# Choice of experts: its steps queued behind the low parts of weights, bounds repeated four times, no low part on GpSimd

## The chip, the cores and the metric

One core of one Trainium2 chip runs the whole program. The metric is device time in microseconds, the median of the runs: 1494.61 us before (three runs, 1493.63 to 1494.88).

## The reference, cut to what matters

Two residual blocks on 256 tokens of width 1024, in float32. The first has a token mixer and then `peer`, a layer that picks 16 of 16384 experts for each token and each of 8 heads. The change lies in `peer`:

```python
q = (ht @ wq).reshape(T, P_HEADS, 2, P_DKH)
s = jnp.einsum('thcd,hcnd->thcn', q, subkeys).astype(jnp.float32)
s1, i1 = lax.top_k(s[:, :, 0], P_TOPK)
s2, i2 = lax.top_k(s[:, :, 1], P_TOPK)
cand = (s1[..., :, None] + s2[..., None, :]).reshape(T, P_HEADS, P_TOPK * P_TOPK)
sc, ci = lax.top_k(cand, P_TOPK)
e = take_along_axis(i1, ci // P_TOPK) * N_KEYS + take_along_axis(i2, ci % P_TOPK)
g = jax.nn.softmax(sc, axis=-1)
# a = gelu(u[e] . h) * g ;  out = sum of a * v[e]
```

The kernel does not gather rows of u and v. It multiplies the tokens with all of u, weighs every expert by the sum of its g (zero for one that was not picked), and multiplies with all of v.

## The kernel before, in words

**Weights.** A float32 product is made as three matmuls of float32r halves: high weight by high input, high weight by low input, low weight by high input (`mm3`, lines 185 to 187). Weights come in by SP's DMA queue as 1 MB pieces `raw` (line 152, three buffers), each of two chunks of 128 x 1024. `split` (lines 160 to 167) makes a chunk's high part `wh` on ACT (line 165) and its low part `wl` = raw - wh on DVE (line 166), or on GpSimd for the chunks listed in `pool_`. In this stretch there are four buffers of each of wh and wl, in a ring. One chunk is 24 matmuls of 128x256 (`gemm`).

**The stretch that the change touches.** The input hh, hl is finished by `modulated` (lines 349, 342, 343) while `gemms` multiplies the first three chunks of u with it (lines 220, 221, 225). Then, for four groups hq of two heads, `queries(hq)` multiplies four chunks of wq (none for the first group, done earlier), copies the product to qT (lines 1022, 1026) and makes two tiles of scores `scs` by 16 matmuls (line 1030) and two ACT copies (line 1033; three buffers). After each group come seven chunks of u (`z_chunks`, up to chunk 28), and then the chunks up to ZR = 50. Each of these ends in a GELU on ACT (line 871). From chunk 50 on, the next background work (`weights_of`, lines 1043 to 1073) needs the chosen indices.

**The choice of experts** runs on DVE beside these chunks, as one generator `routing()`. For each of the eight score tiles, `route` does four steps of MAX8, FIND_INDEX8, MATCH_REPLACE8, MAX8, FIND_INDEX8 (lines 883 to 888), one step that makes 54 candidates a head (lines 895, 899), and two steps like the first four on the candidates (lines 905 to 910). After each second group, `select` turns positions into indices for 128 tokens and four heads: it compares with 16 bounds (`reached`, line 931), multiplies with steps (line 940) or sizes (line 947), and adds up 16 values in four halvings (`total`, lines 936, 937). `spread` makes the softmax (ACT Exp, line 971), turns indices and weights by PE (lines 984, 987) and writes idxT and gT.

**The order.** The program is traced in the order of the code, and a planner then sets each engine's queue by its own costs and the order of tracing; it may put a step that is ready ahead of instructions that were traced before it. `advance` traces NR = 1.6 steps of the generator after each chunk of u, whatever a step takes. `tc.issue_after(ins)` makes what is traced inside it on the engine of `ins` follow `ins` in that engine's queue.

The chunks of u with even numbers below 50 have their low part on GpSimd:

```python
cu = chunks(a["uT"], range(64), pool_={*range(0, 50, 2)})
```

Of the kernel before, what the change touches and what calls it, by code (L numbers as in the profile page):

```python
# [10 lines left out]
F16 = mybir.dt.float16  # L11
# [3 lines left out]
ALU = mybir.AluOpType  # L15
# [20 lines left out]
F2 = 10  # L36
KA = 0
KB = 2
NZ, NR, NW, ZR, NX, NY = (7, 1.6, 1.4, 50, 1.05, 1.05)

# [26 lines left out]
def constants():  # L69
    c = {t: np.zeros((128, n), np.float32) for t, n in NCST.items()}  # L70

    def at(n):
        t, a, w = CST[n]
        return c[t][:, a:a + w]

    p = np.arange(128)
    at("ident")[:] = np.eye(128)
    at("mneg")[:] = np.where(p[:, None] <= p[None, :], 0.0, NEG)
    at("mneg2")[:] = np.where(p[:, None] < p[None, :], 0.0, NEG)
    at("tri")[:] = np.where(p[:, None] >= p[None, :], 1.0, 0.0)  # L80

    at("eh")[:, [7, 39]] = 1.0
    for h in range(8):
        at("dup")[64 + h, [h, 32 + h]] = 1.0
        at("sel")[[h, 32 + h], h] = 1.0
    for i in range(2):
        at("e2")[64 * i:64 * i + 64, [38 + i, 102 + i]] = 1.0
        for m in range(8):
            r = 32 * (m // 4) + 2 * (m % 4) + i
            at("sel2")[[r, 64 + r], 2 * m + i] = 1.0  # L90
    i16 = np.repeat(np.arange(128), TB)[None, :].repeat(128, 0).astype(np.float16)
    start, size = np.zeros(16), np.zeros(16)
    start[1:8] = np.cumsum([n for _, n in RUNS])[:7]
    start[8:] = sum(n for _, n in RUNS) + np.arange(8)
    size[1:] = np.diff(start)
    pick = np.stack([start, size, np.arange(16)])[None].repeat(128, 0).astype(np.float16)
    return c, np.ascontiguousarray(i16), pick.reshape(128, 3 * 16)


class Banks:  # L100
# [12 lines left out]
def body(ctx: ExitStack, tc: tile.TileContext, a: dict):  # L113
# [46 lines left out]
    def split(raw, on=V, by=A):  # L160
        sps.append(sps.pop(0))
        n = sps.count(sps[0])
        wh = sps[0].tile([128, 1024], F32R, tag="wh", name="wh", bufs=n)
        wl = sps[0].tile([128, 1024], F32R, tag="wl", name="wl", bufs=n)
        by.copy(wh, raw) if by is A else by.tensor_copy(wh, raw)  # L165
        on.tensor_sub(wl, raw, wh)  # L166
        return wh, wl

    def chunks(src, blocks, ready=(), late={}, pool_=()):

# [192 lines left out]
    def advance(gens, n=1):  # L363
        due[0] += n
        for _ in range(int(due[0])):
            due[0] -= 1
            while gens:
                try:
                    next(gens[0])
                    break  # L370
                except StopIteration:
                    gens.pop(0)

    def drain(gens):
        while gens:
# [37 lines left out]
    with ExitStack() as p1:  # L413
# [149 lines left out]
        bg = []  # L563
# [268 lines left out]
    with ExitStack() as p2:  # L832
# [43 lines left out]
        def route(t, hq, st):  # L876

            sc = st
            tv = rp.tile([128, 4, 16], F32, tag="tv", name="tv", bufs=2)
            ti = i12[t].rearrange("p h c k -> p (h c) k")[:, 4 * hq:4 * hq + 4]  # L880
            for i in range(4):
                s1 = sc[:, i * 128:(i + 1) * 128]
                V.max(out=tv[:, i, 0:8], in_=s1)
                V.max_index(out=ti[:, i, 0:8], in_max=tv[:, i, 0:8], in_values=s1)
                rep = rp.tile([128, 128], F32, tag="rep", name="rep", bufs=2)
                V.match_replace(out=rep, in_to_replace=tv[:, i, 0:8], in_values=s1, imm_value=-3e38)
                V.max(out=tv[:, i, 8:16], in_=rep)
                V.max_index(out=ti[:, i, 8:16], in_max=tv[:, i, 8:16], in_values=rep)
                yield
            tv2 = tv.rearrange("p (h c) k -> p h c k", c=2)  # L890
            cand = rp.tile([128, 2, NC50], F32, tag="cand", name="cand", bufs=2)
            o = 0
            for lo, hi in GROUPS:
                m, n = hi - lo, 16 // (lo + 1)
                V.tensor_add(cand[:, :, o:o + m * n].rearrange("p h (a b) -> p h a b", a=m),
                             tv2[:, :, 0, lo:hi, None].to_broadcast([128, 2, m, n]),
                             tv2[:, :, 1, None, 0:n].to_broadcast([128, 2, m, n]))
                o += m * n
            V.tensor_add(cand[:, :, o:o + 8], tv2[:, :, 0, 8:16], tv2[:, :, 1, 0:1].to_broadcast([128, 2, 8]))
            yield  # L900
            cv = gw[t][:, 2 * hq:2 * hq + 2, :]
            ci = pos[t][:, 2 * hq:2 * hq + 2, :]
            for i in range(2):
                s1 = cand[:, i, :]
                V.max(out=cv[:, i, 0:8], in_=s1)
                V.max_index(out=ci[:, i, 0:8], in_max=cv[:, i, 0:8], in_values=s1)
                rep = rp.tile([128, 128], F32, tag="rep", name="rep", bufs=2)
                V.match_replace(out=rep[:, :NC50], in_to_replace=cv[:, i, 0:8], in_values=s1, imm_value=-3e38)
                V.max(out=cv[:, i, 8:16], in_=rep[:, :NC50])
                V.max_index(out=ci[:, i, 8:16], in_max=cv[:, i, 8:16], in_values=rep[:, :NC50])  # L910
                yield

        def select(t, q):

# [7 lines left out]
            V.tensor_copy(cf, pos[t][:, hs, :].rearrange("p h k -> p k h"))  # L922
            V.tensor_copy(st[:, :, 0], tf[:, :, 0])
            V.tensor_sub(st[:, :, 1:16], tf[:, :, 1:16], tf[:, :, 0:15])
            yield
            m = rp.tile([128, 16, 16, 4], F16, tag="m", name="m", bufs=1)
            pr = rp.tile([128, 16, 16, 4], F16, tag="pr", name="pr", bufs=1)
            mf, pf = (v_.rearrange("p a k h -> p a (k h)") for v_ in (m, pr))

            def reached(at, v_):  # L930
                V.tensor_tensor(out=mf, in0=v_.rearrange("p k h -> p (k h)")[:, None, :].to_broadcast([128, 16, 64]),
                                in1=pick[:, at, :, None].to_broadcast([128, 16, 64]), op=ALU.is_ge)

            def total(out):
                for n in (8, 4, 2):
# [4 lines left out]
                V.tensor_tensor(out=pr, in0=m, in1=st[:, c, :, None, :].to_broadcast([128, 16, 16, 4]), op=ALU.mult)  # L940

            reached(0, cf)
            steps(0)
            yield
            total(fi[t][:, 0, 64 * q:64 * q + 64])
            yield
            V.tensor_tensor(out=pf, in0=mf, in1=pick[:, 1, :, None].to_broadcast([128, 16, 64]), op=ALU.mult)
            rk = rp.tile([128, 16, 4], F16, tag="rk", name="rk", bufs=2)
            total(rk.rearrange("p k h -> p (k h)"))
            yield  # L950
            V.tensor_sub(cf, cf, rk)
            reached(2, cf)
            steps(1)
            yield
            total(fi[t][:, 1, 64 * q:64 * q + 64])
            yield

        pick = rp.tile([128, 3, 16], F16, name="pick")
        A.dma_start(out=pick, in_=a["pick"].rearrange("p (c a) -> p c a", c=3))
        i12 = [rp.tile([128, 8, 2, 16], U32, name=f"i12{t}") for t in range(2)]  # L960
        pos = [rp.tile([128, 8, 16], U32, name=f"pos{t}") for t in range(2)]
        fi = [rp.tile([128, 2, 128], F32, name=f"fi{t}") for t in range(2)]
# [4 lines left out]
        def spread(t):  # L967
# [8 lines left out]
            for q in range(2):  # L976
                hs = slice(4 * q, 4 * q + 4)
                V.tensor_mul(gp[:, q].rearrange("p k h -> p h k"), ex[:, hs],
                             sm[:, 1, hs, None].to_broadcast([128, 4, 16]))
            yield  # L980
            ts_ = slice(t * 128, (t + 1) * 128)
            pt = gt()[:, :256]
            for i in range(2):
# [5 lines left out]
            A.activation(gs, pg[:, 0:128], AF.Copy, scale=GS)  # L989
            V.tensor_copy(gT[:, ts_, 0], gs)  # L990
            V.tensor_sub(gT[:, ts_, 1], gs, gT[:, ts_, 0])
            yield

        def routing():
            for hq in range(4):
# [14 lines left out]
        def queries(hq):  # L1010
            qT = rp.tile([128, 4, 256], F32, tag="qT", name="qT", bufs=1)
            for i in range(4):
                if hq == 0:
                    stack = ExitStack()
                    if i == 0:
                        stack.enter_context(tc.issue_after(made.ins))
                    wb = rp.tile([128, 1], F32, tag="wb", name="wb", bufs=2)
                    V.tensor_reduce(out=wb, in_=pss[i][:, 256:258], axis=AX.X, op=ALU.add)
                    stack.close()
                    u = m2.tile([128, 256], F32, tag="u", name="u", bufs=2)  # L1020
                    V.tensor_mul(u, pss[i][:, :256], r2)
                    A.activation(qT[:, i, :], u, AF.Identity, bias=wb)
                    continue
                ps = mmt()
                gemm(ps, next(cq), h2h, h2l)
                A.copy(qT[:, i, :], ps)
            for t in range(2):
                ps = gt()
                for i in range(4):
# [43 lines left out]
                                           scalar=1.0 / GS, in1=zz, op0=ALU.mult, op1=ALU.mult)  # L1073
                yield

        cu = chunks(a["uT"], range(64), pool_={*range(0, 50, 2)})
        ce = chunks(a["ev"], range(64))

        def z_chunks(i0, i1, bg=(), n=1):
            w = next(cu)  # L1080
            for i in range(i0, i1):
                w1 = next(cu) if i + 1 < i1 else None
                z_chunk(i, w)
                advance(bg, n)
                w = w1

        steps = []
# [15 lines left out]
        for hq in range(4):  # L1103
            queries(hq)
            if hq == 0:
                for i in range(3):
                    z_chunk(i, None, psz[i])
            z_chunks(max(3, NZ * hq), NZ * hq + NZ, bgr, NR)
        z_chunks(4 * NZ, ZR, bgr, NR)
        drain(bgr)  # L1110
        rst.close()
        op_ = pool("op", stack=p2)
# [425 lines left out]
```

## Time and profile before

| | before |
|---|---|
| median of three runs | 1494.61 us |
| the profiled execution | 1493.74 us, of which its span is 1491.9 us |
| busy: PE, PE weight loads, DVE, ACT, GpSimd | 96%, 88%, 77%, 61%, 7% of the span |
| mean granted TensorE clock | 0.983 |
| low parts of weights on DVE and on GpSimd | 415 and 35 |

The profile is of one execution. Busy shares are means over stages with different limits, so the stretch from about 343 us (the input's last step) to 558 us (chunk 50 of u) is read by itself. L166 is line 166 of the kernel; PE is TensorE's matmuls, PEld its weight loads, POOL is GpSimd. A duration of an instruction goes from its start to its last write; two DVE instructions that follow each other can overlap in such records.

### The profile page before, as it was taken

To read this page: it belongs to the slowest core of one execution; us is meant where nothing else is said; L and a number is where in the kernel's file an instruction comes from. 1 tells how busy PE (TensorE), PEld (TensorE's weight loads), DVE (VectorE), ACT (ScalarE), POOL (GpSimd) and SP (SyncE) were. 2 spreads that over 40 slices of the span, in tenths; PEclk is the share of its full clock that TensorE was granted. 3 is DMA by queue.
4 is the path that set the end of the run, shared out by engine and by line. 5 is a ranking of instruction groups with operands and counts; after the bars stand their busy time and mean duration, and the time that the engine had idled before them with its cause. 6 is when DMAs were issued, how large, how long until landed. Compare 5 with 4: busy or idle time off the path is not lost.

```text
span 1491.9 us, 27112 instructions
## 1 busy us (share of the span) xinstructions
PE 1435.5 (96%) x10998; PEld 1318.5 (88%) x10998; DVE 1151.9 (77%) x2159; ACT 913.7 (61%) x1288; POOL 106.0 (7%) x55
## 2 busy tenths in 40 slices
PE   4899999998989899999999999999999999999998
PEld 4889999988989899999778998777788799899897
DVE  8978997677998838878999887888855679565554
ACT  3554565445434448888777777777754579554442
POOL 3310000022232330000000000000000000000000
PEclk6999999999999999999999999999999999999999
DMA  9457695543534455444455455555555544345452
GB/s 347 182 185 264 236 351 204 194 146 123 178 131 170 150 189 170 156 166 160 156 183 172 170 170 173 175 177 173 179 173 194 200 156 142 113 171 197 170 171 84
DMA packets 40016, 268.64 MB, mean 180 GB/s; under 512 B 4561, under 2 KB 5329, under 8 KB 9170
## 3 DMA queue, kind: packets, MB, share of 16 engines
q1 hardware_dynamic: 38882, 264.67, 51.1%
q10 hardware_dynamic: 1008, 2.23, 0.5%
q8 instruction: 86, 1.41, 0.4%
q14 instruction: 40, 0.33, 0.1%
HBM read 265.83 MB, written 1.05 MB: 179 GB/s over the span
## 4 chain that ended last, share of the span: by engine, by line
PE 81%; DVE 12%; ACT 3%; DMA 2%; issue 1%; SPq 0%; DVEq 0%; ACTq 0%
PE mm L185 13%; PE mm L187 13%; PE mm L186 13%; PE acc L256 10%; PE acc L257 10%; PE acc L258 10%; PE g L1069 3%; DVE wl L166 2%; DMA araw<-in_wada_dram 2%; DVE pr L936 1%; PE acc L185 1%; PE acc L187 1%; PE acc L186 1%; ACT wh L165 1%; DVE scr L429 1%
## 5 line engine op out<-in xcount | busy, mean ns | idle before, releaser
L165 ACT CAST wh<-raw 128x1024 fp32r<-128x1024 f32 x450 | 471.2, 1050 | 442.1 <-PE mm L186 205.2
L166 DVE TENSOR_TENSOR wl<-raw,wh 128x1024 fp32r<-128x1024 f32 x415 | 508.7, 1228 | 182.1 <-ACT wh L165 177.8
L187 PE MATMUL mm<-hh,wl 128*128 128x256 f32 x1816 | 514.4, 283 | 10.6 <-DVE wl L166 10.6
L185 PE MATMUL mm<-hh,wh 128*128 128x256 f32 x1816 | 519.5, 286 | 3.2 <-ACT z L871 3.2
L186 PE MATMUL mm<-hl,wh 128*128 128x256 f32 x1816 | 512.1, 282 | 0.0
L187 PEld LDWEIGHTS mm<-hh,wl 128*128 128x128 f32 x1816 | 345.2, 190 | 11.6 <-DVE wl L166 11.4
L185 PEld LDWEIGHTS mm<-hh,wh 128*128 128x128 f32 x1816 | 344.3, 190 | 6.1 <-ACT z L871 3.8
L186 PEld LDWEIGHTS mm<-hl,wh 128*128 128x128 f32 x1816 | 344.7, 190 | 1.1
L256 PE MATMUL acc<-wh,ah 128*128 128x512 f32 x512 | 205.0, 401 | 1.0 <-ACT ah L263 1.0
L257 PE MATMUL acc<-wh,al 128*128 128x512 f32 x512 | 201.8, 394 | 0.0
L258 PE MATMUL acc<-wl,ah 128*128 128x512 f32 x512 | 201.6, 394 | 0.0
L1047 ACT COPY o<-os 128x1024 f16<-128x1024 f16 x96 | 197.0, 2053 | 1.2 <-DVE os L1044 1.2
L166 POOL TENSOR_TENSOR wl<-raw,wh 128x1024 fp32r<-128x1024 f32 x35 | 89.4, 2560 | 421.3 <-PE mm L327 239.0
L258 PEld LDWEIGHTS acc<-wl,ah 128*128 128x128 f32 x512 | 96.2, 188 | 22.3
L256 PEld LDWEIGHTS acc<-wh,ah 128*128 128x128 f32 x512 | 96.1, 188 | 21.7 <-ACT ah L263 1.1
L257 PEld LDWEIGHTS acc<-wh,al 128*128 128x128 f32 x512 | 96.1, 188 | 20.6
L1072 DVE SCALAR_TENSOR_TENSOR z<-g,z 128x256 f32<-128x256 f32 x128 | 51.1, 419 | 45.2 <-PE g L1069 45.0
L1044 DVE TENSOR_TENSOR os<-io,idxT 128x1024 f16<-128x1024 f16 x96 | 66.2, 689 | 21.8 <-ACT o L1047 21.2
L1054 DVE TENSOR_TENSOR og<-o,gT 128x512 f16<-128x512 f16 (+1 forms) x96 | 82.5, 859 | 0.0
L429 DVE SCALAR_TENSOR_TENSOR scr<-araw,crow 128x1024 f32<-128x1024 f32 x48 | 60.4, 1259 | 1.1 <-DMA araw<-in_wada_dram 0.8
L1069 PEld LDWEIGHTS <-o 128*128 128x128 f16 x1536 | 46.4, 96 | 15.6 <-issue 11.9
L1069 PE MATMUL g<-og,o 128*128 128x32 f16 (+1 forms) x1536 | 56.4, 182 | 0.3 <-ACT o L1047 0.3
(437 smaller groups left out, 1952.9 us busy)
## 6 DMA issues: line engine op xcount, KB each, us to landing
raw<-in_uT_dram SPq DMA_DIRECT2D x64, 1024.0 KB, 4.9
raw<-in_ev_dram SPq DMA_DIRECT2D x64, 1024.0 KB, 4.8
araw<-in_wada_dram SPq DMA_DIRECT2D x16, 1024.0 KB, 5.1
raw<-in_wup_dram SPq DMA_DIRECT2D x16, 1024.0 KB, 4.9
raw<-in_wdn_dram SPq DMA_DIRECT2D x16, 1024.0 KB, 4.9
raw<-in_wcxb_dram SPq DMA_DIRECT2D x12, 1024.0 KB, 5.1
araw<-in_wada_dram SPq DMA_DIRECT2D x16, 512.0 KB, 9.9
raw<-in_wout_dram SPq DMA_DIRECT2D x8, 1024.0 KB, 4.9
```

The costliest lines, as they stand in the source:

```text
L165: by.copy(wh, raw) if by is A else by.tensor_copy(wh, raw)
L166: on.tensor_sub(wl, raw, wh)
L185: T.matmul(ps, lhsT=wh, rhs=xh, start=start, stop=False, skip_group_check=skip)
L186: T.matmul(ps[:, :n], lhsT=wh, rhs=xl, start=False, stop=False, skip_group_check=skip)
L187: return T.matmul(ps, lhsT=wl, rhs=xh, start=False, stop=stop, skip_group_check=skip)
L256: T.matmul(acc[t][c], lhsT=xh[:, ts_], rhs=wh[:, cs], start=first and n == 0, stop=False)
L257: T.matmul(acc[t][c], lhsT=xl[:, ts_], rhs=wh[:, cs], start=False, stop=False)
L258: T.matmul(acc[t][c], lhsT=xh[:, ts_], rhs=wl[:, cs], start=False, stop=last and n == len(steps) - 1)
L429: return V.scalar_tensor_tensor(out=scr, in0=raw, scalar=0.5, in1=crow, op0=ALU.mult, op1=ALU.mult, accum_out=ada[:, j:j + 1])
L1047: A.copy(o1, os.rearrange("p n t -> p t n"))
L1054: V.tensor_tensor(out=og, in0=o2[:, :, None, :].to_broadcast([128, TB, 2, m]), in1=gT[:, ts_, :, None].to_broadcast([128, TB, 2, m]), op=A ...
L1069: T.matmul(ps[:, t], lhsT=o1[:, t, :], rhs=og[:, t, i], start=i == 0, stop=i == 1)
```

## The change

Four edits. (1) No low part of u is made on GpSimd: the 25 that were there are made on DVE. (2) The choice's steps are given out by a new function `pace`, after each chunk of u up to 50 and also after each of the 12 chunks of wq. It adds NR = 1.7 us to an account and traces steps until what they are said to take (the value each `yield` now returns) has used it up; a step that waits for scores returns None and ends the round. (3) Each such step's DVE instructions are queued behind the latest low part that DVE makes. (4) The table of bounds `pick` holds each value four times, so that the comparison and the product with sizes read it with four neighbours in memory, in the form of line 940, instead of one value for 64 outputs.

```diff
-NZ, NR, NW, ZR, NX, NY = (7, 1.6, 1.4, 50, 1.05, 1.05)
+NZ, NR, NW, ZR, NX, NY = (7, 1.7, 1.4, 50, 1.05, 1.05)
...
-    pick = np.stack([start, size, np.arange(16)])[None].repeat(128, 0).astype(np.float16)
-    return c, np.ascontiguousarray(i16), pick.reshape(128, 3 * 16)
+    pick = np.stack([start, size, np.arange(16)]).repeat(4, 1)[None].repeat(128, 0).astype(np.float16)
+    return c, np.ascontiguousarray(i16), pick.reshape(128, 3 * 64)
...
-        on.tensor_sub(wl, raw, wh)
+        last = on.tensor_sub(wl, raw, wh)
+        if on is V:
+            low_part[:] = [last]
         return wh, wl
...
+    def pace(gens, us):
+        owed[0] += us
+        while gens and owed[0] > 0:
+            with tc.issue_after(low_part[0].ins):
+                cost = next(gens[0], False)
+            if cost is False:
+                gens.pop(0)
+            elif cost is None:
+                break
+            else:
+                owed[0] -= cost
...
         (route: each first-level step)      yield 1.45
         (route: candidates)                 yield 0.55
         (route: each second-level step)     yield 0.8
         (select, nine steps)                yield 0.75 / 0.6 / 0.6 / 1.1 / 0.6 / 1.1 / 0.8 / 0.6 / 1.1
         (spread, two steps)                 yield 1.3 / 1.0
...
+            def bound(at):
+                return pick[:, at, :, None, :].to_broadcast([128, 16, 16, 4])
             def reached(at, v_):
-                V.tensor_tensor(out=mf, in0=v_.rearrange("p k h -> p (k h)")[:, None, :].to_broadcast([128, 16, 64]),
-                                in1=pick[:, at, :, None].to_broadcast([128, 16, 64]), op=ALU.is_ge)
+                V.tensor_tensor(out=m, in0=v_[:, None].to_broadcast([128, 16, 16, 4]), in1=bound(at), op=ALU.is_ge)
...
-            V.tensor_tensor(out=pf, in0=mf, in1=pick[:, 1, :, None].to_broadcast([128, 16, 64]), op=ALU.mult)
+            V.tensor_tensor(out=pr, in0=m, in1=bound(1), op=ALU.mult)
...
                 gemm(ps, next(cq), h2h, h2l)
                 A.copy(qT[:, i, :], ps)
+                pace(bgr, NR)
...
-        cu = chunks(a["uT"], range(64), pool_={*range(0, 50, 2)})
+        cu = chunks(a["uT"], range(64))
...
-            z_chunks(max(3, NZ * hq), NZ * hq + NZ, bgr, NR)
-        z_chunks(4 * NZ, ZR, bgr, NR)
+            z_chunks(max(3, NZ * hq), NZ * hq + NZ, bgr, NR, pace)
+        z_chunks(4 * NZ, ZR, bgr, NR, pace)
```

## Rows read from the trace of the kernel before

**Rows 1.** The page, chain that ended last, by engine.
```profile
PE 81%; DVE 12%; ACT 3%; DMA 2%; issue 1%; SPq 0%; DVEq 0%; ACTq 0%
```
**Rows 2.** Busy time by stretch: us, then PE, PEld, DVE, ACT, POOL (instructions), clock, DMA.
```profile
362.40:387.90 25.50, 25.50 (x216) 25.36 (x216) 23.64 (x113) 14.07 (x22) 7.04 (x3) 1.00 0.51 170
387.90:463.70 75.80, 69.49 (x563) 68.19 (x562) 70.61 (x274) 31.28 (x50) 19.04 (x8) 0.98 0.45 155
463.70:515.20 51.50, 43.54 (x343) 42.92 (x342) 50.88 (x169) 24.70 (x35) 18.72 (x8) 0.94 0.36 122
515.20:558.10 42.90, 42.90 (x359) 42.77 (x357) 12.59 (x12) 19.46 (x29) 11.98 (x5) 0.99 0.63 218
...
380.00:400.00 20.00, 20.00 (x170) 19.86 (x169) 18.62 (x101) 9.90 (x16) 7.52 (x3) 1.00 0.58 203
```
**Rows 3.** Waits of PE, 342 to 562 us: total, times, longest.
```profile
PE mm L187 <- DVE wl L166: 10.6, 4, 5.5
...
PE mm L185 <- ACT z L871: 3.2, 2, 2.5
```
**Rows 4.** The timeline where GpSimd's low parts meet DVE: start, us.
```profile
344.21 5.15 DVE L343 SCALAR_TENSOR_TENSOR hl<-u,prm,hh 128x256 fp32r<-128x256 f32 x2 [0.48 <-ACT hh L342]
344.23 4.86 POOL L166 TENSOR_TENSOR wl<-raw,wh 128x1024 fp32r<-128x1024 f32 x2 [8.00 <-ACT hh L342]
...
355.86 0.89 DVE L343 SCALAR_TENSOR_TENSOR hl<-u,prm,hh 128x256 fp32r<-128x256 f32 x2 [0.26 <-ACT hh L342]
...
508.74 2.34 POOL L166 TENSOR_TENSOR wl<-raw,wh 128x1024 fp32r<-128x1024 f32 x1 [3.43 <-ACT wh L165]
508.77 3.38 DVE L931 TENSOR_TENSOR m<-cf,pick 128x1024 f16<-128x1024 f16 x1
...
513.35 0.58 PE L187 MATMUL mm<-hh,wl 128*128 128x256 f32 x1 [5.47 <-DVE wl L166]
```
**Rows 5.** Groups of 362 to 565 us, by shape: busy us, mean ns.
```profile
L166 DVE TENSOR_TENSOR wl<-raw,wh 128x1024 fp32r<-128x1024 f32 x40 | 51.6, 1294 | 31.4 <-ACT wh L165 31.4
...
L931 DVE TENSOR_TENSOR m<-cf,pick 128x1024 f16<-128x1024 f16 x8 | 11.9, 1488 | 0.1
L936 DVE TENSOR_TENSOR pr<-pr 128x512 f16<-128x512 f16 x12 | 11.3, 940 | 0.2
...
L936 DVE TENSOR_TENSOR pr<-pr 128x256 f16<-128x256 f16 x12 | 7.8, 653 | 0.2
L940 DVE TENSOR_TENSOR pr<-m,st 128x1024 f16<-128x1024 f16 x8 | 7.5, 938 | 0.1
```
**Rows 6.** Lines of DVE, 362 to 565 us: duration ns min/median/max.
```profile
L166 DVE TENSOR_TENSOR wl<-raw,wh x40: 1201/1217/3426, 364.8 to 562.1; 128x1024 fp32r<-128x1024 f32 x40
...
L931 DVE TENSOR_TENSOR m<-cf,pick x8: 1203/1218/3385, 405.4 to 508.8; 128x1024 f16<-128x1024 f16 x8
...
L940 DVE TENSOR_TENSOR pr<-m,st x8: 668/680/2744, 407.7 to 513.2; 128x1024 f16<-128x1024 f16 x8
...
L947 DVE TENSOR_TENSOR pr<-m,pick x4: 1210/1224/1227, 411.0 to 506.0; 128x1024 f16<-128x1024 f16 x4
```
**Rows 7.** DVE's timeline where nothing of GpSimd runs: start, us.
```profile
437.32 0.40 DVE L936 TENSOR_TENSOR pr<-pr 128x512 f16<-128x512 f16 x1
...
437.91 0.28 DVE L936 TENSOR_TENSOR pr<-pr 128x256 f16<-128x256 f16 x1
...
438.83 0.48 DVE L883 MAX8 tv<-scs 128x8 f32<-128x128 f32 x2
...
440.01 0.27 DVE L887 MAX8 tv<-rep 128x8 f32<-128x128 f32 x1
440.21 1.20 DVE L166 TENSOR_TENSOR wl<-raw,wh 128x1024 fp32r<-128x1024 f32 x1
441.33 0.08 DVE L888 MATCH_VALUE_LOAD i<-tv,rep 128x8 f32 x1
441.40 0.28 DVE L888 FIND_INDEX8 i<-tv,rep 128x8 uint32<-128x128 f32 x1
```
**Rows 8.** Waits of DVE, 362 to 516 us: total, times, longest.
```profile
DVE tv L883 <- ACT scs L1033: 7.3, 3, 3.2
```

More of the change, by code (lines that the diff above doesn't have):

```diff
@@ L165, in split @@
         by.copy(wh, raw) if by is A else by.tensor_copy(wh, raw)
-        on.tensor_sub(wl, raw, wh)
+        last = on.tensor_sub(wl, raw, wh)
+        if on is V:
+            low_part[:] = [last]
         return wh, wl
+    low_part = []
     def chunks(src, blocks, ready=(), late={}, pool_=()):
@@ L372, in advance @@
                     gens.pop(0)
+    owed = [0.0]
+    def pace(gens, us):
[9 more added lines that the diff above has]
+                owed[0] -= cost
     def drain(gens):
@@ L888, in route @@
                 V.max_index(out=ti[:, i, 8:16], in_max=tv[:, i, 8:16], in_values=rep)
-                yield
+                yield 1.45
             tv2 = tv.rearrange("p (h c) k -> p h c k", c=2)
@@ L899, in route @@
             V.tensor_add(cand[:, :, o:o + 8], tv2[:, :, 0, 8:16], tv2[:, :, 1, 0:1].to_broadcast([128, 2, 8]))
-            yield
+            yield 0.55
             cv = gw[t][:, 2 * hq:2 * hq + 2, :]
@@ L910, in route @@
                 V.max_index(out=ci[:, i, 8:16], in_max=cv[:, i, 8:16], in_values=rep[:, :NC50])
-                yield
+                yield 0.8
         def select(t, q):
@@ L924, in select @@
             V.tensor_sub(st[:, :, 1:16], tf[:, :, 1:16], tf[:, :, 0:15])
-            yield
+            yield 0.75
             m = rp.tile([128, 16, 16, 4], F16, tag="m", name="m", bufs=1)
             pr = rp.tile([128, 16, 16, 4], F16, tag="pr", name="pr", bufs=1)
-            mf, pf = (v_.rearrange("p a k h -> p a (k h)") for v_ in (m, pr))
+            pf = pr.rearrange("p a k h -> p a (k h)")
+            def bound(at):
+                return pick[:, at, :, None, :].to_broadcast([128, 16, 16, 4])
             def reached(at, v_):
-                V.tensor_tensor(out=mf, in0=v_.rearrange("p k h -> p (k h)")[:, None, :].to_broadcast([128, 16, 64]),
-                                in1=pick[:, at, :, None].to_broadcast([128, 16, 64]), op=ALU.is_ge)
+                V.tensor_tensor(out=m, in0=v_[:, None].to_broadcast([128, 16, 16, 4]), in1=bound(at), op=ALU.is_ge)
             def total(out):
@@ L942, in select @@
             reached(0, cf)
+            yield 0.6
             steps(0)
-            yield
+            yield 0.6
             total(fi[t][:, 0, 64 * q:64 * q + 64])
-            yield
-            V.tensor_tensor(out=pf, in0=mf, in1=pick[:, 1, :, None].to_broadcast([128, 16, 64]), op=ALU.mult)
+            yield 1.1
+            V.tensor_tensor(out=pr, in0=m, in1=bound(1), op=ALU.mult)
+            yield 0.6
             rk = rp.tile([128, 16, 4], F16, tag="rk", name="rk", bufs=2)
             total(rk.rearrange("p k h -> p (k h)"))
-            yield
+            yield 1.1
             V.tensor_sub(cf, cf, rk)
             reached(2, cf)
+            yield 0.8
             steps(1)
-            yield
+            yield 0.6
             total(fi[t][:, 1, 64 * q:64 * q + 64])
-            yield
-        pick = rp.tile([128, 3, 16], F16, name="pick")
-        A.dma_start(out=pick, in_=a["pick"].rearrange("p (c a) -> p c a", c=3))
+            yield 1.1
+        pick = rp.tile([128, 3, 16, 4], F16, name="pick")
+        A.dma_start(out=pick, in_=a["pick"].rearrange("p (c a h) -> p c a h", c=3, a=16))
         i12 = [rp.tile([128, 8, 2, 16], U32, name=f"i12{t}") for t in range(2)]
@@ L979, in spread @@
                              sm[:, 1, hs, None].to_broadcast([128, 4, 16]))
-            yield
+            yield 1.3
             ts_ = slice(t * 128, (t + 1) * 128)
@@ L991, in spread @@
             V.tensor_sub(gT[:, ts_, 1], gs, gT[:, ts_, 0])
-            yield
+            yield 1.0
         def routing():
@@ L1074, in weights_of, with z_chunks @@
                 yield
-        cu = chunks(a["uT"], range(64), pool_={*range(0, 50, 2)})
+        cu = chunks(a["uT"], range(64))
         ce = chunks(a["ev"], range(64))
-        def z_chunks(i0, i1, bg=(), n=1):
+        def z_chunks(i0, i1, bg=(), n=1, by=advance):
             w = next(cu)
@@ L1083, in z_chunks @@
                 z_chunk(i, w)
-                advance(bg, n)
+                by(bg, n)
                 w = w1
```

## The prediction

> **What bounds the kernel now.** I read the chain of waits first: PE holds 81% of it and DVE 12% [rows 1], so the kernel ends when PE ends, except where DVE keeps PE waiting. The busy time by stretch shows where that is. Between 515 and 558 us, and in the 20 us from 380, PE is busy throughout; between 388 and 515 us PE is idle for 6.3 and 8.0 us and its clock falls to 0.98 and 0.94 of full, while DVE is busy for 70.6 of 75.8 and 50.9 of 51.5 us [rows 2]. After 515 us it is the other way round: the choice of experts is nearly over and DVE is busy for 12.6 of 42.9 us. So DVE's work lies at the wrong time more than there is too much of it. PE's waits name what was late: the low parts, 10.6 us in four waits, the longest 5.5 us [rows 3]. The timeline shows why DVE was late. A comparison of 1.22 us takes 3.38 us when it starts 0.03 us behind a low part on GpSimd, and the low part that is queued behind it holds PE for 5.47 us [rows 4]. The same happens at 344 us: two steps of the input that take 0.89 us together elsewhere take 5.15 us beside two low parts on GpSimd.
>
> **PE's time for the stretch from 362.4 to 558.1 us.** It is 195.7 us for 216 + 563 + 343 + 359 = 1481 instructions. At the pace of the undisturbed 20 us, 20.0 / 170 = 0.1176 us each [rows 2], they need 174.2 us. What a DVE that is never late could give back here is 195.7 - 174.2 = 21.5 us. This holds the slower clock too, since the rate comes from a stretch at full clock (2.4 GHz).
>
> **DVE's time for the same stretch after the change**, part by part.
>
> *Low parts.* The stretch has 59 chunks (47 of u, 12 of wq). On DVE an undisturbed low part takes 1.12 us from its start to the next one's (441.33 - 440.21, [rows 7]) and 1.22 us by itself [rows 6]: 66 to 72 us, taken as 68. Some 23 of these 59 are the ones that come over from GpSimd; they cost DVE 23 x 1.15 = 26 us.
>
> *What GpSimd cost DVE.* Mean against undisturbed duration: low parts 40 x (1.294 - 1.217) = 3.1 us; L931 8 x (1.488 - 1.218) = 2.2; L936 of 512 elements 12 x (0.940 - 0.40) = 6.5, of 256 12 x (0.653 - 0.28) = 4.5; L940 8 x (0.938 - 0.680) = 2.1 [rows 5 to 7]. That is 18.4 us at least, of which 15.3 us on the choice. It goes with GpSimd's low parts, so edit 1 adds about 8 us net.
>
> *Bounds four times.* L931 (eight) and L947 (four) take the form of L940: 16-bit operands whose last four elements are neighbours. L940 takes 0.680 us for 1024 elements where they take 1.22 [rows 6]. 12 x 0.54 = 6.5 us saved; 0 if the form doesn't help. The table is loaded once and grows from 96 to 384 bytes a partition, on ACT's queue far ahead of its use: nothing.
>
> *The choice itself.* From 362.4 to 515.2 us DVE is busy for 145.1 us [rows 2]; 29 low parts of 1.12 us and their 3.1 us of disturbance take 35.6, which leaves 109.5. Less 15.3 and 6.5 that is 87.7, and about 2 us of copies behind 515 us make 90. This is with steps of several tiles interleaved, as now: two MAX8 take 0.48 us together, where one takes 0.27 [rows 7]. Behind the low part of each chunk only one or two steps stand, so a step may have to wait for the one before it. Then each instruction costs its whole duration, about 0.08 us more (1.20 against 1.12; two of 0.28 in 0.48), except the 144 loads of match values, whose successor starts 0.07 us behind a load of 0.08 us. The stretches hold 113 + 274 + 169 - 29 = 527 such instructions; 383 x 0.08 = 31 us more: 121 us at most. The change's own table of step times sums to 8 x 7.95 + 4 x 7.25 + 2 x 2.3 = 97.2 us, nearer the lower end; I take 97.
>
> Sum: 68 + 97 = 165 us, ends 156 and 193, against PE's 174. Each chunk takes PE 24 x 0.1176 = 2.82 us, and a low part with 1.7 us of steps fills just that. The 59 calls give out 100.3 us, so the steps end some two chunks ahead of chunk 50. Four buffers let DVE run up to three chunks (8.5 us) ahead, which covers a step of 1.45 us that overshoots.
>
> *Waits at DVE's head.* Now DVE waits 7.3 us in all for scores [rows 8]. With pacing the choice lags behind: when the scores of group 1 come, 8 calls have given out 13.6 of 15.9 us; for group 2, 32.3 of 46.3; for group 3, 51.0 of 62.2. So DVE has work whenever scores are late, and I cost this at nothing. Without that cover a wait is at most 3.2 us.
>
> *Start.* At 344 us the input's step no longer meets GpSimd: 5.15 - 0.89 = 4.3 us less on the path to PE. The two low parts come to DVE in the same place, 2 x 1.12 = 2.2 us. Gain 2.0 us (4.3 if they fit in gaps).
>
> *What stays or is late next.* PE's 3.2 us of waiting for GELU outputs, two times, with ACT's Exp and its table [rows 3], stays inside the 21.5: less 3.2. At the end PE transposes indices that in the present order were ready 40 us earlier; now they are ready about two chunks ahead. I take 2 us for that and for clock lost behind stalls, between 0 and 6. ACT's 1.4 us a chunk and the weights' DMA (0.63 busy at PE's full rate, [rows 2]) have room; GpSimd's queue only gets emptier.
>
> **Sum.** 21.5 + 2.0 - 3.2 - 2 = 18.3 us less. The profiled execution took 1493.74 us, 0.9 less than the median: 1475.4, or a median of 1476.
>
> **Rivals.**
> 1. *DVE becomes the bound.* Steps run one behind the other at their full durations, and the 121 us hold: 72 + 115 to 121 = 187 to 193 us, gain 195.7 - 187 = 9 us or less, plus 2 at the start less 1 at the end: about 1485 (1481 to 1492). For: only one or two steps stand behind each low part, and a halving in `total` needs the one before it. Against: the low part and two independent steps can fill the gaps. The Trainium skill has a rule that says it flatly (VectorE: DVE Perf Modes, The DRAIN you can't avoid): the next DVE instruction does not start until the pipe of the one before is empty. By it the time would be 1485; the trace as it stands disagrees, since the second of two MAX8 overlaps the first by 0.08 us.
> 2. *The order does not change as meant.* The planner puts steps of the choice, or the low parts, in bunches all the same. Then only GpSimd's disturbance and the bounds are gained and half of PE's 21.5 us stays lost: 1494 - 11 = 1484. For: the planner ran the choice 40 us ahead of the transposes before. Against: each step now has a low part that it can't pass.
> 3. *Slower: scores stand at DVE's head.* A step that is queued behind a low part and waits for its score tile holds up every low part behind it, and the choice no longer has other tiles' steps to fill in. Eight tiles at 3.2 us [rows 8] are 26 us, against 23.5 to gain: 1494.6 + 2 = 1497. It decides from 2.9 us a tile on. Against: the lag worked out above, which leaves at most the first tiles without cover.
> 4. *More than forecast*: the end and the GELU waits go too, 1471.
>
> **Chances.** Forecast 0.55 (its own range 1470 to 1481), rival 1 0.22, rival 2 0.09, rival 3 0.05, rival 4 0.09. The two unknown costs, the choice at 90 to 121 us and the end at 0 to 6 us, carry the time from 1470 to 1492; the range leaves out the last of rival 1 and rival 3: 1468 to 1488. Faster by over 0.2% (3 us, about what a measurement tells from no change) 0.92, the same 0.04, slower 0.04.
>
> **What would show it.** In the trace after: no low part on GpSimd between 340 and 560 us; L931 and L947 at 0.68 us and no DVE instruction of this stretch over 1.3 us; PE busy throughout, with waits for wl under 3 us in all; chunk 50 at about 537 to 540 us instead of 558; DVE evenly busy at 90 to 95% up to there. A DVE at 100% and PE waiting for wl chunk after chunk would make it rival 1; DVE standing at L883 for ACT's scores, rival 3. A span that shrinks in any other stretch would mean that I read the wrong place.

## The result, and the profile after

The changed kernel takes 1472.07 us (median of four runs, 1470.94 to 1472.39) against 1494.12 us of the kernel before in the same comparison: ratio 0.9853, 95% interval 0.9841 to 0.9865, 22 us less. The forecast was 1476 (1468 to 1488): the time lies in the range, 4 us under the point. In each of two later runs, `no_gpsimd_bounds` and `after_again`, one execution fell in a slower state of the chip (granted clock 0.65 and 0.85), and the medians given for them are of the other three.

The page after, busy time and the chain that ended last, by engine, against [rows 1]:

```profile
PE 1428.5 (97%) x10998; PEld 1312.4 (89%) x10998; DVE 1152.7 (78%) x2184; ACT 913.8 (62%) x1288; POOL 41.9 (3%) x30
...
PE 89%; DVE 6%; ACT 3%; DMA 2%; issue 1%; SPq 0%; DVEq 0%; ACTq 0%
```

DVE's share of the chain is halved, though DVE does 25 instructions more and is busy as long as before. The same stretches as in [rows 2], columns as there:

```profile
362.40:387.90 25.50, 25.50 (x217) 25.36 (x216) 24.70 (x115) 11.84 (x19) 0.00 (x0) 1.00 0.61 208
387.90:463.70 75.80, 75.80 (x640) 75.51 (x639) 70.18 (x273) 35.38 (x54) 0.00 (x0) 1.00 0.52 175
463.70:515.20 51.50, 51.50 (x437) 51.50 (x436) 47.46 (x159) 27.02 (x40) 0.00 (x0) 1.00 0.53 176
515.20:558.10 42.90, 42.12 (x403) 41.73 (x402) 33.76 (x60) 32.66 (x38) 0.00 (x0) 1.00 0.54 185
```

PE is busy without a break up to 515 us and its clock stays at full (2.4 GHz); by 515.2 us it has done 1294 instructions where it had done 1122. PE's waits between 342 and 562 us, against [rows 3]:

```profile
PE mmz L225 <- DVE hl L347: 2.5, 4, 0.7
PE g L1011 <- DVE gp L1002: 0.8, 1, 0.8
```

No wait for a low part is left, and none for a GELU. Lines of DVE from 362 to 565 us (duration ns min/median/max), against [rows 6]; L953 is the old L931:

```profile
L166 DVE TENSOR_TENSOR wl<-raw,wh x69: 1203/1219/1227, 362.3 to 563.1; 128x1024 fp32r<-128x1024 f32 x69
...
L953 DVE TENSOR_TENSOR m<-cf,pick x8: 680/689/693, 411.0 to 519.4; 128x1024 f16<-128x1024 f16 x8
```

Nothing is stretched any more, and the new form of the bounds takes 0.69 us, in L969 (the old L947) too. One row of PE, the products of the first three chunks with the low weights, marks the end of the start; of before (L225), then of after (L229):

```profile
L225 PE MATMUL mmz<-hh,wl x24: 277/281/287, 357.6 to 360.3; 128*128 128x256 f32 x24
```
```profile
L229 PE MATMUL mmz<-hh,wl x24: 277/281/287, 353.3 to 356.0; 128*128 128x256 f32 x24
```

It ends 4.3 us earlier. Of that 1.9 us come from ahead of the change and are scatter between executions: the last sums in front of this step start at 337.9 us in the profile after and at 339.9 before, but also at 339.9 in the run `old_bounds` below, whose time is the same as the changed kernel's. A measure without this scatter goes from these last sums to the first matmul into `acc`, the product with v behind the choice: 366.8 us before (339.9 to 706.7) and 345.5 after (337.9 to 683.4). So 21.3 of the 22 us are gained there. The runs below are compared by it too, as the time from the sums to `acc`.

### The profile page after: what moved, and what is told of

Read it like the earlier page. It is cut to its first block, busy times and chain, and to the rows that moved or that the text cites. A ratio compares the mean times of both kernels' runs of the same rounds, so it can differ in the third digit from the quotient of the medians.

```text
span 1470.3 us, 27107 instructions
## 1 busy us (share of the span) xinstructions
PE 1428.5 (97%) x10998; PEld 1312.4 (89%) x10998; DVE 1152.7 (78%) x2184; ACT 913.8 (62%) x1288; POOL 41.9 (3%) x30
## 4 chain that ended last, share of the span: by engine, by line
PE 89%; DVE 6%; ACT 3%; DMA 2%; issue 1%; SPq 0%; DVEq 0%; ACTq 0%
PE mm L189 15%; PE mm L191 15%; PE mm L190 15%; PE acc L260 10%; PE acc L261 10%; PE acc L262 10%; PE g L1094 3%; DMA araw<-in_wada_dram 2%; DVE wl L166 1%; PE acc L189 1%; PE acc L191 1%; PE acc L190 1%; ACT wh L165 1%; DVE scr L448 1%; PE mm L225 1%
## 5 line engine op out<-in xcount | busy, mean ns | idle before, releaser
L166 DVE TENSOR_TENSOR wl<-raw,wh 128x1024 fp32r<-128x1024 f32 x440 | 536.7, 1222 | 161.1 <-ACT wh L165 155.7
L268 DVE TENSOR_TENSOR al<-z,ah 128x256 fp32r<-128x256 f32 x128 | 53.5, 420 | 3.1 <-ACT ah L267 3.1
```

What stands on the lines that cost most here:

```text
L166: last = on.tensor_sub(wl, raw, wh)
```

## The experiments

Theory A is what stood in the prediction: DVE's work comes late, and GpSimd's hold on DVE, the bounds and the order of the steps each give a part. Theory B: the hold alone. Theory C: the order alone. Each run is compared with the kernel before in the same job (medians 1492.9 to 1493.3 us).

**Edit 1 alone** (`no_gpsimd`, and again as `no_gpsimd_again`), on the kernel before:

```diff
-        cu = chunks(a["uT"], range(64), pool_={*range(0, 50, 2)})
+        cu = chunks(a["uT"], range(64))
```

> The kernel before with edit 1 alone: all low parts of u on DVE, steps still given out by count. Theory A (DVE's work is late; the lock, the bounds and the pacing each give part of it): DVE gains some 18 us of disturbance and gets 26 us of low parts, the choice still runs early, so PE still loses about 20 us there; the start gains 2.4 us: 1492, between 1487 and 1498. Theory B (GpSimd's hold on DVE is nearly all of it): 1476 or less. Theory C (the order of the steps is nearly all of it): 1494 or more.

Measured: 1474.26 us, ratio 0.9876 (0.9860 to 0.9892). This is theory B's number, a little better than its limit of 1476, and far from theory A's 1492. The page's DVE time did not rise by 8 us, it is unchanged:

```profile
PE 1428.3 (97%) x10998; PEld 1312.2 (89%) x10998; DVE 1151.7 (78%) x2184; ACT 913.8 (62%) x1288; POOL 42.0 (3%) x30
```

Its last sum of the choice starts at 501.9 us, where it started at 515.0 before. From the first MAX8 of the choice to that sum (columns as in rows 2), before, then with edit 1 alone:

```profile
362.90:515.25 152.35, 138.08 (x1114) 136.02 (x1113) 145.18 (x555) 69.55 (x104) 44.80 (x17) 0.97 0.43 147
```
```profile
358.65:502.20 143.55, 141.04 (x1171) 140.25 (x1170) 141.91 (x574) 72.39 (x107) 0.00 (x0) 0.99 0.49 169
```

The choice starts 4.3 us earlier, of which 1.9 are again scatter, and takes 8.8 us less. Of these DVE's busy time gives only 3.3 us, since it now makes 48 low parts there instead of 29. The rest is idle time of DVE, most of it waits for scores: 2.5 us instead of the 7.3 of [rows 8]. What the 17 low parts on GpSimd cost DVE is read from `gpsimd_fill` below, where DVE's queue stays the same.

For PE much changes, though DVE's time on the page is equal: no wait for a low part is left, and between 340 and 565 us its idle time falls from 18.9 to 5.5 us and its granted clock rises from 0.97 to 0.99. From the sums to `acc` that makes 348.4 us instead of 366.8.

**Edit 4 alone** (`bounds`: the table and the two comparisons and products as in the change, on the kernel before).

> The kernel before with edit 4 alone: bounds held four times. Theory A: DVE is the bound while the choice runs, so the 6.5 us that twelve instructions save come through: 1488, between 1486 and 1491. Theories B and C: no change, 1493 to 1495. In the trace the comparison should take 0.68 us instead of 1.22 where GpSimd does not hold it.

Measured: 1488.25 us, ratio 0.9967 (0.9954 to 0.9979). The number is theory A's, 4.8 us less. It is not shown that these are 4.8 of the 6.5 us: DVE's busy time falls by 8.7 us (1143.2 against 1151.9), and in this order 12 of its instructions between 342 and 565 us, not 14, take over 1.3 us beside GpSimd's.

**Edits 1 and 4 together, no pacing** (`no_gpsimd_bounds`).

> Edits 1 and 4, without the pacing. Theory A: the sum of the two alone, about 1486 (1481 to 1491), so that pacing is worth the remaining 14 us. Theory B: 1474 or less. Theory C: 1490 or more.

Measured: 1477.03 us, ratio 0.9894 (0.9874 to 0.9913). All three were missed: the two gains of 19 and 5 us do not add, and the time is some 3 us above edit 1 alone. Only about 1 us of that lies where the bounds act: 349.5 us from the sums to `acc`, against 348.4 and 348.6 in two executions of edit 1 alone. The profiled execution lost 1.6 us more between 1168 and 1300 us, at a granted clock of 0.99, as one of those two did. PE waits 3.1 us once for a copy of qT, which stands in ACT's queue behind a high part that waits 4.7 us for its weights:

```profile
PE g L1032 <- ACT qT L1028: 3.1, 1, 3.1
ACT wh L165 <- DMA raw<-in_uT_dram: 4.7, 1, 4.7
```

With edit 1 alone the same two waits are 2.1 and 3.7 us. With other DVE times the planner sets another order. Why it comes out worse was not taken further.

**The changed kernel without the edge to the low part** (`no_edge`):

```diff
-            with tc.issue_after(low_part[0].ins):
-                cost = next(gens[0], False)
+            cost = next(gens[0], False)
```

> The changed kernel without the edge that queues each step behind the latest low part; the steps are still traced by their DVE time. Theory A: the planner again runs the choice early, as it did before, and PE waits for low parts: 1484 (1479 to 1489), with several us of PE waiting for wl. Theory B: 1472 to 1474. A variant of theory C, that tracing by time is enough: 1472 to 1474, with DVE's busy share even up to chunk 50.

Measured: 1477.15 us, ratio 0.9892 (0.9875 to 0.9908), between the two, and with none of the waits for wl that theory A named: PE's one long wait is 2.8 us for qT, as in the run before, and its granted clock is 0.83 from 450 to 460 us, around that wait, where it is 1.00 in the changed kernel. The edge is worth 5 us (349.9 against 345.5 from the sums to `acc`), by another wait than I thought.

**The changed kernel with GpSimd's low parts back** (`gpsimd_back`, the line of edit 1 undone).

> The changed kernel with every second low part of u up to chunk 50 on GpSimd again (edit 1 undone); steps stay paced, behind the latest low part that DVE makes. Theory A: DVE's sum for the stretch falls from about 165 to 157 us, below PE's 174, so the disturbances of 2 us each are mostly covered by buffers that run ahead; the start loses its 2.4 us and a few us more are lost: 1478 (1474 to 1483). Theory B: 1487 or more. Theory C: 1474 or less.

Measured: 1479.77 us, ratio 0.9920 (0.9907 to 0.9934). Theory A's 1478 (1474 to 1483). Undoing edit 1 costs 8 us here. Without pacing edit 1 is worth 19 us with the old bounds, but 11 with the new ones, which this kernel has (`bounds` 1488.25 against `no_gpsimd_bounds` 1477.03). So pacing shields from some 3 of 11 us, not from most of the hold.

**The changed kernel with the old bounds** (`old_bounds`, edit 4 undone).

> The changed kernel with the table of bounds as before (edit 4 undone): DVE has 6.5 us more in a stretch where it was busy for 93% of the time. Theory A: covered, PE stays the bound: 1472 to 1475. Rival: DVE was so near to being the bound that the 6.5 us come through: 1477 to 1479.

Measured: 1471.88 us, ratio 0.9856 (0.9841 to 0.9871). Covered: in the changed kernel the bounds are worth nothing. PE is the bound.

**Every step as soon as it is ready** (`all_at_once`, on the changed kernel):

```diff
-NZ, NR, NW, ZR, NX, NY = (7, 1.7, 1.4, 50, 1.05, 1.05)
+NZ, NR, NW, ZR, NX, NY = (7, 20.0, 1.4, 50, 1.05, 1.05)
```

> The changed kernel with 20 us instead of 1.7 us of steps after each chunk: every step is given out as soon as its scores are there, behind the low part of that moment; no GpSimd, new bounds. The same instructions as in the changed kernel. Theory A: the choice comes in bunches, DVE stands in front of low parts and PE waits for them: 1484 (1478 to 1492). Theory B: 1472 to 1474, since the order plays no part.

Measured: 1506.24 us, ratio 1.0087 (1.0073 to 1.0100): slower than before, and beyond what any theory gave. The same instructions as in the changed kernel cost 34 us more when the order puts them in bunches ahead of low parts. PE's waits there:

```profile
PE mm L191 <- DVE wl L166: 14.3, 4, 5.8
PE g L1008 <- DVE fi L958: 4.5, 1, 4.5
```

and one of its stretches, in which PE stands for 7.0 us and the granted clock falls to 0.79 (from 480 to 500 us it stands for 7.9 us, and the clock is 0.74):

```profile
356.00:380.00 24.00, 17.02 (x119) 16.42 (x118) 19.97 (x114) 9.21 (x17) 0.00 (x0) 0.79 0.22 74
```

So the order can decide, but edit 1 alone had not been in need of it. That left open whether in the kernel before the hold or its order was at work. The next two runs separate them.

**The order of before, without the hold** (`gpsimd_fill`): on the kernel before, GpSimd writes zeros for the low part of the 25 chunks instead of subtracting (`G.memset` in place of `on.tensor_sub`), which leaves out the product with those low parts. DVE's queue is the same, instruction for instruction.

```diff
-        on.tensor_sub(wl, raw, wh)
+        if on == "fill":
+            G.memset(wl.bitcast(F32), 0.0)
+        else:
+            on.tensor_sub(wl, raw, wh)
```

> The kernel before with one thing changed: for the 25 chunks of u, GpSimd fills the low part with zeros (it writes and reads nothing) instead of subtracting. It leaves out the product with the low part of those chunks; PE does the same matmuls, and DVE's queue is the same, instruction for instruction, as in the kernel before. Theory B (GpSimd's hold on DVE is nearly all of it): DVE loses its 21 to 28 us of disturbance, PE waits little: 1471 to 1478. Theory A, as it stands after four runs (the order in which the choice stands ahead of low parts costs by itself): 1482 to 1488.

Measured: 1471.25 us, ratio 0.9853 (0.9837 to 0.9870). The whole gain, with the old order, the old bounds and no pacing. The same 2159 DVE instructions take 1125.3 us instead of 1151.9:

```profile
PE 1430.5 (97%) x10998; PEld 1313.1 (89%) x10998; DVE 1125.3 (77%) x2159; ACT 914.0 (62%) x1288; POOL 65.9 (4%) x55
```

26.6 us is then what the 25 subtractions on GpSimd cost DVE. The same for the choice alone, to be set against the 145.18 us of the same 555 instructions before:

```profile
358.30:490.55 132.25, 130.46 (x1092) 129.34 (x1091) 122.54 (x555) 68.51 (x102) 14.36 (x15) 1.00 0.49 169
```

That is 22.6 us for 17 subtractions, 1.3 us each: more than the 1.12 us for which DVE makes a low part itself. Instruction by instruction, only 14 of the 2159 are longer in the kernel before by more than 0.3 us: by 0.9 to 2.2 us, together 27.7. Each of them has two inputs in SBUF, runs beside a subtraction of GpSimd, and ends only after it. The other 11 subtractions stretched nothing. Five ran while DVE was idle. The rest met almost only instructions with one input, such as MAX8, and at 358.9 us two products with an input in PSUM (0.42 us each, as in the changed kernel).

Two fills and the DVE instructions that start beside them follow (start, duration), cut:

```profile
405.71 1.03 DVE L926 COPY st<-tf 128x8 f16<-128x8 f16 x1
405.75 0.96 POOL L167 MEMSET wl<- 128x1024 f32 x1 [15.72 <-PE mm L190]
...
456.35 0.96 POOL L167 MEMSET wl<- 128x1024 f32 x1 [7.05 <-PE mm L190]
456.55 0.25 DVE L898 TENSOR_TENSOR cand<-tv 128x16 f32<-128x16 f32 x2
```

No instruction with two inputs is stretched at 456 us. At 405.7 us one fill does delay DVE: a copy of 0.16 us takes 1.03 and ends as the fill ends, and two short instructions with two inputs that start behind it end with it (0.96 and 0.83 us instead of 0.22). It is the only such place among the 25 fills; whether those two were held themselves or by the copy ahead of them is not shown. The comparison, still in its old form, takes what it took at best before (min/median/max):

```profile
L934 DVE TENSOR_TENSOR m<-cf,pick x8: 1206/1220/1224, 400.8 to 486.2; 128x1024 f16<-128x1024 f16 x8
```

The Trainium skill (SBUF — State Buffer, Who interferes with whom) says that a DVE instruction with two SBUF inputs contends with a GpSimd instruction that reads SBUF, and not with one that only writes. These two runs agree: two-input instructions of DVE are stretched to 3.4 us by the subtractions [rows 4, 6] and, but for the two behind the copy at 405.7 us, not by the fills. What the run does not separate: a fill is also shorter than a subtraction and does not wait for the high part. PE had no wait for a low part of GpSimd's before [rows 3], so little can come from there.

**The hold, on top of edit 1** (`gpsimd_extra`): DVE makes all low parts, and GpSimd does its 25 subtractions too, into a tile that nothing reads.

```diff
-        on.tensor_sub(wl, raw, wh)
+        if on == "both":
+            V.tensor_sub(wl, raw, wh)
+            G.tensor_sub(spare_[0], raw, wh)
+        else:
+            on.tensor_sub(wl, raw, wh)
```

> Edit 1 alone (all low parts of u on DVE), and GpSimd does its 25 subtractions too, into a scratch tile that nothing reads. DVE's queue is that of edit 1 alone but for one pair. Theory B: the hold comes back on top of the 28 us of low parts, DVE is over PE's time: 1490 (1483 to 1500), with single DVE instructions of 2 to 3.4 us in the trace. Theory A: the order of edit 1 is what gave the gain, with every low part in DVE's own queue: 1474 to 1478.

Measured: 1507.46 us, ratio 1.0093 (1.0077 to 1.0110): 34 us more than edit 1 alone in the same job (1473.90), for work that nobody waits for: between 340 and 570 us no wait of the trace ends with one of these subtractions. Theory B, and more of it than it gave. The page's DVE time is 38 us longer, and low parts on DVE reach 3.4 us:

```profile
PE 1443.5 (96%) x10998; PEld 1324.8 (88%) x10998; DVE 1189.7 (79%) x2184; ACT 913.9 (61%) x1288; POOL 114.0 (8%) x55
```

The line of the 25 subtractions on DVE (min/median/max, first to last):

```profile
L167 DVE TENSOR_TENSOR wl<-raw,wh x25: 1202/1215/3418, 343.2 to 557.1; 128x1024 fp32r<-128x1024 f32 x25
```

**What pacing is worth** (`after_again` and `no_gpsimd_again` in one job).

> The changed kernel once more, beside edit 1 alone, to see whether the pacing is worth anything on top of edit 1: 1471 to 1473. If pacing is worth what the first runs show, 1.5 to 3 us below edit 1 alone.

> Edit 1 alone once more, in the same job as the changed kernel: 1474 (1473 to 1475.5). If the earlier difference was the scatter between jobs, 1472 to 1473.

Measured: 1472.11 us (0.9835 to 0.9874) and 1473.90 us (0.9853 to 0.9886). The changed kernel is about 2 us ahead of edit 1 alone. The intervals overlap, but in both jobs together the changed kernel takes 1470.9 to 1472.4 us and edit 1 alone 1473.7 to 1475.7. From the sums to `acc` the difference is 3 us, twice: 345.5 in both traces of the changed kernel, 348.4 and 348.6 with edit 1 alone, where PE waits 2.1 and 2.3 us for a copy of qT.

**Two more low parts off GpSimd** (`wq_low_dve`): the low parts of two chunks of wq, at 323 us, go to DVE as well.

```diff
-LA = ('nnre',(2,3))
+LA = ('nnre',())
```

> The changed kernel with the low parts of two chunks of wq on DVE instead of GpSimd. In the changed kernel two additions of the residual at 323 us take 3.95 us together beside these two low parts, where two take 0.75 us alone, and DVE is then on the chain that ended last. If that hold on DVE costs PE time as at 344 us in the kernel before: 3.2 us saved, up to 2.2 us spent on the two low parts: 1470.5 (1468.5 to 1471.5). If PE's own fill work or the low parts hide it: 1472 to 1473.

Measured: 1471.49 us, ratio 0.9853 (0.9838 to 0.9868): not told apart from the changed kernel by its time. The trace shows a gain in the step itself: from DVE's reciprocal (L327) at 323.0 us, 321.2 in the changed kernel, to the last sums 15.1 us pass, where it is 16.7 to 17.1 in every other run. This execution came to the step 1.8 us later, which is scatter, so the sums start at 338.1 us, almost as in the changed kernel (337.9). No run here beat the changed kernel clearly.

## Why the prediction was right, and where not

**PE's time as the limit: right.** 174.2 us were worked out for 1481 instructions; after the change PE does its 1294 instructions up to 515.2 us in 152.8 us, 0.1181 us each, without a break. `old_bounds`, with 5 us more of busy time on DVE (1158.0 against 1152.7) and the same time, shows that DVE is not the bound. The forecast's total rests on this limit alone and not on which edit keeps DVE from being late. So it came out although 19 of the 22 us are edit 1's alone, which the prediction did not see; in that it was lucky.

**The size: low by 4 us, in one term.** "What stays or is late next" took off 3.2 us for GELU waits and 2 for the end. GELU waits are gone and the end costs one wait of 0.8 us. The longer GELU wait (2.5 us, at 485.7 us) hung on DVE as well: before, ACT stood with its Exp 4.5 us in two waits until DVE had the softmax's input (traces between 340 and 562 us), after, 1.3 us. The other (0.7 us, at 437.4) came behind a high part that had waited 5.3 us for its weights. Rival 4 (1471) was this case. The start gave 2.4 us where 2.0 were forecast.

**The step that failed: "so edit 1 adds about 8 us net".** The hold was counted from the groups that showed it most, as "18.4 us at least", and then used as if it were the whole. With the 4.3 us at the start that made 22.7; it is 26.6 us of DVE's busy time (`gpsimd_fill`), and 1.3 us for each low part made while the choice ran. Left out were the held instructions of two more groups, L895 (two) and L937 (one), 5.4 us. So edit 1 costs DVE nothing over the kernel (1151.7 against 1151.9), where the prediction had 8 us more. The choice ends 13 us earlier with it (501.9 against 515.0): it starts 4.3 us earlier, DVE's busy time in it is 3.3 us less, and DVE's idle time 5.5 us less. The waits for scores [rows 8], which the prediction left to the pacing, fell from 7.3 to 2.5 us without it; why was not separated.

**"DVE's work lies at the wrong time more than there is too much of it": wrong for the kernel before.** On this rested theory A's 1492 us for edit 1 alone, missed by 18 us. `gpsimd_fill` keeps DVE's queue as it was and has the whole gain, so the order of before was good enough once nothing held DVE. `all_at_once` shows that a bad order costs even more than the hold did (34 us); before's was not such an order. Pacing adds some 2 us to edit 1, and the edge is needed with it (`no_edge` 1477).

**Bounds: the saving right, its worth not.** 12 x (1.22 - 0.69) = 6.4 us of DVE time, as forecast. With them the kernel before is 4.8 us faster, with two held instructions fewer as well; in the changed one, where PE is the bound, they give nothing.

**The choice at 97 us between 90 and 121: right in kind.** DVE's page time is 1152.7 us in the changed kernel and 1146.8 with the same instructions freely ordered (`no_gpsimd_bounds`): standing behind one low part costs about 6 us of overlap, not 31. Rival 1 would have shown DVE without a pause and PE waiting for low parts; neither is there. The rule of the Trainium skill that stood beside it (VectorE: DVE Perf Modes, The DRAIN you can't avoid) is not as flat as the prediction has it: the same paragraph adds that "A next op that is not held starts earlier". The overlaps of 0.08 us [rows 7] agree with that addition. Rival 2 did not come: without the edge the time is 1477, with it 1472. Rival 3 was not seen: no wait for scores at DVE's head between 362 and 516 us.

## What to carry to other kernels

Work that is moved to GpSimd to relieve DVE should be priced by what it does to DVE's other instructions: here one subtraction on GpSimd (2.3 to 3.4 us) cost DVE 1.3 us on average while the choice ran, and the same subtraction on DVE 1.12 us. Count the hold over all groups (sum of mean minus undisturbed duration), or measure it by replacing the GpSimd instruction with one that reads nothing; even that one held a copy once, at 405.7 us. And before an order is blamed for a late engine, keep the order and take away what stretches its instructions.

## What was not expected of the hardware

25 GpSimd subtractions whose results nothing reads made the kernel 34 us slower (`gpsimd_extra` against edit 1 alone), since they delay single DVE instructions by up to 2.2 us (3.42 against 1.22 us). The hold is rare and long: 14 of 2159 DVE instructions before, about 2 us each. Of the 25 GpSimd fills of such a tile (0.96 us), one delayed DVE, by 0.9 us, at a copy. And saving DVE 6.4 us need not save time: edits 1 and 4 together are no faster than edit 1 alone.
